# A sparse 3x3 convolution whose stores leave by two queues, one image each, with whole-pair loads and no tiny loads

## The chip, the cores and the metric

The kernel runs on one core of one Trainium2 chip. A core has five engines that run side by side: TensorE (PE in the profile, its weight loads PEld), VectorE (DVE), ScalarE (ACT), GpSimd (POOL) and SyncE (SP). Sixteen DMA engines carry data between the chip's memory (HBM) and the core's on-chip memory. SyncE, ScalarE and GpSimd can each issue transfers, by queues of their own. The metric is the device time of one execution in microseconds, taken as the median of several runs; one further execution is recorded by the hardware profiler, and all rows shown here come from such records.

## The reference

Sixteen images of 64 channels and 64x64 points are convolved with 128 filters of 3x3, padded by one. The weights are drawn with nine tenths of them zero, and the reference skips those; the kernel does the whole dense product.

```python
batch, c_in, h, w, c_out, k = 16, 64, 64, 64, 128, 3
x_pad = np.pad(x, ((0, 0), (0, 0), (1, 1), (1, 1)))
output[b, co] += weight[co, ci, kh, kw] * x_pad[b, ci, kh:kh+h, kw:kw+w]
```

The input is 16.8 MB of float32, the output 33.6 MB.

## The kernel before, in words

**Pairs and blocks.** Two images make a pair: 64 channels of each fill the 128 partitions. There are eight pairs (`NP`), and each is worked on in four blocks of 16 output rows (`BLOCKS`, `ROWS`), 32 blocks in all (`N`). Even and odd output rows of a block are formed from three partial products in the manner of Winograd along the rows: one product of `sums` (row pairs added), which both share, goes to `ps[0]`; one of `odd` to `ps[1]`; one of `even` to `ps[2]` or `ps[3]`. Each product is a run of matmuls with 64-row halves, one half for each image.

**Who does what.** GpSimd issues the loads of pairs (line 105; they turn float32 into bf16 on the way), then for each block adds row pairs (`fill_sums`, line 183) and copies the even rows (`fill_even`, line 172). ScalarE copies the shared product out of `ps[0]` into `pc` (line 280) and then the next block's odd rows (`fill_odd`, lines 163 and 164). VectorE adds `pc` to `ps[1]` and to `ps[2]` or `ps[3]` and so writes the even and odd output rows (lines 293 and 297) into one of four output buffers, `outs[p % 4]`. TensorE runs a loop over two blocks at a time (line 337 has all its products). Everything is ordered by semaphores set by hand: `s_pe` counts products, `s_pc` copies, `s_out` finished blocks, `s_x[p]` landed loads and `s_st[p]` landed stores of pair `p`.

**Loads.** The first 32 rows of pair 0 go by SyncE (line 94) beside the weights (line 91). The rest of pair 0 and pairs 1, 2 and 7 are one transfer each. Pairs 3 to 6 are three transfers: 59 to 62 of the rows, and the last two to five rows in two pieces divided by channel (`LOADS`). GpSimd issues pairs 0, 1, 2 and the first piece of pair 3 ahead of its blocks, and then one transfer from the list `todo` behind every filling step.

**Tiny loads.** SyncE waits until pair 2 has landed, then issues fifteen loads of 1 to 15 rows of 36 to 92 bytes of the weights into `spare`, which nothing reads (`marks`, line 305). It does so again behind pair 4's store (`MARKED`).

**Stores.** No store goes out before the load of pair 6 (`GATE`) has landed. Then SyncE goes through the pairs: it waits for a pair's four blocks and issues one 4 MB store with both images (line 320). Pairs 6 and 7 go in halves of 32 rows (`HALVED`); the last half of pair 7 is issued behind the section (line 370). Before VectorE writes pair `p` into a buffer again it waits until the store of pair `p - 4` has landed (line 290).

Of the kernel before, what the change touches and what calls it, by code (L numbers as in the profile page):

```python
# [7 lines left out]
FP32 = mybir.dt.float32  # L8
# [9 lines left out]
BLOCKS = 4  # L18
# [4 lines left out]
def kernel(  # L23
# [6 lines left out]
    nc = tc.nc  # L30
    B, C_IN, H, W = x.shape
    C_OUT, _, KH, KW = weight.shape
    assert (B, C_IN, H, W) == (16, 64, 64, 64) and (C_OUT, KH, KW) == (128, 3, 3)
    NP = B // 2
    HEAD = 32
    N = NP * BLOCKS
    GATE = 6
    HALVED = (6, 7)
    MARKED, MARKS = 4, tuple(range(1, 16))

    def sbuf(name, shape, dtype):
        return nc.alloc_sbuf_tensor(name, shape, dtype).ap()

    def sem(name):
        return nc.alloc_semaphore(name)

    def pair(p):
        return x[2 * p : 2 * p + 2].rearrange("n i h w -> (n i) h w")
# [5 lines left out]
    xs = [  # L54
        home[:, 1 + p, :].bitcast(BF16).rearrange("c (h w) -> c h w", w=W)
        for p in range(3)
    ]
    xs += [sbuf(f"x{p}", [128, H, W], BF16) for p in range(3, NP)]
    outs = [sbuf(f"o{k}", [C_OUT, 2, H, W], FP32) for k in range(3)]
# [1 line left out]
    w_sb = sbuf("w_sb", [C_OUT, C_IN * KH * KW], FP32)  # L61
    w_bf = sbuf("w_bf", [C_OUT, 3, 4 * C_IN], BF16)
    wT = sbuf("wT", [128, 5, 3, C_OUT], BF16)
    spare = sbuf("spare", [16, 2, 16, 32], FP32)
    ident = sbuf("ident", [128, 128], BF16)
    idle_rhs = sbuf("idle_rhs", [128, 512], BF16)
    zeros = idle_rhs[:, 0:W]
# [9 lines left out]
    s_x = [sem(f"s_x{p}") for p in range(NP)]  # L77
    s_st = [sem(f"s_st{p}") for p in range(NP)]
    s_dve, s_act, s_id, s_tr = sem("s_dve"), sem("s_act"), sem("s_id"), sem("s_tr")
    s_sum, s_even = ([sem(f"s_{n}{k}") for k in range(UNROLL)] for n in ("sum", "even"))  # L80
    s_odd, s_free, s_mark = sem("s_odd"), sem("s_free"), [sem(f"s_mark{i}") for i in range(2)]
    s_pe, s_pc, s_out = sem("s_pe"), sem("s_pc"), sem("s_out")

    def into(p, a, b):
        return out[2 * p : 2 * p + 2].rearrange("n o h w -> o n h w")[:, :, a:b, :]
# [8 lines left out]
    nc.sync.dma_start(out=x_head, in_=pair(0)[:, 0:HEAD, :]).then_inc(s_head, 16)  # L94

    LOADS = {p: [(0, H, 0, 128)] for p in range(NP)}
    LOADS[0] = [(HEAD, H, 0, 128)]
    for p, a, cut in ((3, 62, 120), (4, 60, 88), (5, 59, 117), (6, 61, 119)):  # L100
        LOADS[p] = [(0, a, 0, 128), (a, H, 0, cut), (a, H, cut, 128)]

    def load(p, i=0):
        a, b, c, d = LOADS[p][i]
        nc.gpsimd.dma_start(out=xs[p][c:d, a:b, :], in_=pair(p)[c:d, a:b, :]).then_inc(s_x[p], 16)  # L105

    load(0)
    nc.gpsimd.memset(ident, 0.0).then_inc(s_id, 1)
    nc.gpsimd.wait_ge(s_id, 1)
    nc.gpsimd.affine_select(  # L110
        out=ident,
        in_=ident,
# [8 lines left out]
    def source(p, r):  # L121
        if r < 0 or r >= H:
            return None, None
        if p == 0 and r < HEAD:
            return x_head, (s_head, 16)
        return xs[p], (s_x[p], 16 * len(LOADS[p]))

    def rows_of(k, first, count):

        p = k // BLOCKS  # L130
        pieces = []
        for i, r in enumerate(range(first, first + 2 * count, 2)):
            src, landed = source(p, r)
            if pieces and pieces[-1][2] is src:
                pieces[-1][1] += 1
                pieces[-1][4].append(landed)
            else:
                pieces.append([i, 1, src, r, [landed]])
        return sorted(pieces, key=lambda q: q[2] is not None)
# [3 lines left out]
    def wait(engine, s, value):  # L143
        key = (engine.engine, s.name)
        if waited.get(key, 0) < value:
            engine.wait_ge(s, value)  # L146
            waited[key] = value

    def fill(engine, copy, zero, tile_, k, first, count, done):
        for i, c, src, r, landed in rows_of(k, first, count):  # L150
            if src is None:
                last = zero(tile_[:, i, :])
            else:
                for s in landed:
                    wait(engine, *s)
                last = copy(tile_[:, i : i + c, :], src[:, r : r + 2 * c - 1 : 2, :])
        last.then_inc(done, 1)

    def fill_odd(k, engine=None, copy=None, zero=None, done=None):
        r0 = ROWS * (k % BLOCKS)  # L160
        fill(
            engine or nc.scalar,
            copy or (lambda o, i: nc.scalar.copy(out=o, in_=i)),  # L163
            zero or (lambda o: nc.scalar.copy(out=o, in_=zeros)),
            odd[k % UNROLL], k, r0 - 1, HALF + 1, done or s_odd,
        )
# [10 lines left out]
    def fill_sums(k, engine=nc.gpsimd):  # L177
        p, b = divmod(k, BLOCKS)
        r0 = ROWS * b
        src = source(p, r0)[0]  # L180
        for r in (r0, r0 + ROWS - 1):
            wait(engine, *source(p, r)[1])
        engine.tensor_tensor(  # L183
            out=sums[k % UNROLL],
            in0=src[:, r0 : r0 + ROWS : 2, :],
            in1=src[:, r0 + 1 : r0 + ROWS : 2, :],
            op=ADD,
        ).then_inc(s_sum[k % UNROLL], 1)
# [14 lines left out]
    v = nc.vector  # L203
# [21 lines left out]
    a = nc.scalar  # L225
# [35 lines left out]


    g = nc.gpsimd
    for p in (1, 2):
        load(p)
    todo = [(p, i) for p in range(3, NP) for i in range(len(LOADS[p]))]
    load(*todo.pop(0))
    for k in range(1, N):
        for fill_in, product in ((fill_sums, 2), (fill_even, 6)):
            if k >= UNROLL:  # L270
                wait(g, s_pe, 6 * (k - UNROLL) + product)
            fill_in(k)
            if todo:
                load(*todo.pop(0))


    fill_odd(0)
    for k in range(N):
        wait(a, s_pe, 6 * k + 2)
        a.copy(out=pc[k % 3], in_=ps[0]).then_inc(s_pc, 1)  # L280
        if k + 1 < N:
            fill_odd(k + 1)


    for k in range(N):
        p, b = divmod(k, BLOCKS)
        o = outs[p % 4]
        r0 = ROWS * b
        if p >= 4:
            wait(v, s_st[p - 4], 16)  # L290
        wait(v, s_pc, k + 1)
        wait(v, s_pe, 6 * k + 4)
        v.tensor_tensor(  # L293
            out=o[:, :, r0 : r0 + ROWS : 2, :], in0=ps[1], in1=pc[k % 3], op=ADD
        ).then_inc(s_free, 1)
        wait(v, s_pe, 6 * k + 6)
        v.tensor_tensor(  # L297
            out=o[:, :, r0 + 1 : r0 + ROWS : 2, :], in0=ps[2 + k % 2], in1=pc[k % 3], op=ADD
        ).then_inc(s_out, 1)


    s = nc.sync
    def marks(i, landed):
        for k in MARKS:
            s.dma_start(
                out=spare[0:k, i, k, 0 : 8 + k],
                in_=weight.rearrange("o i kh kw -> o (i kh kw)")[0:k, 0 : 8 + k],
            ).then_inc(landed, 16)

    s.wait_ge(s_x[2], 16)  # L310
    marks(0, s_mark[0])
    s.wait_ge(s_x[GATE], 16 * len(LOADS[GATE]))
    for p in range(NP):
        parts = 2 if p in HALVED else 1
        rows = H // parts
        for h in range(parts):
            if (p, h) == (NP - 1, 1):
                continue
            s.wait_ge(s_out, BLOCKS * p + BLOCKS // parts * (h + 1))
            s.dma_start(  # L320
                out=into(p, rows * h, rows * (h + 1)),
                in_=outs[p % 4][:, :, rows * h : rows * (h + 1), :],
            ).then_inc(s_st[p], 16)
        if p == MARKED:
            marks(1, s_mark[1])


    def tap(g, kw, n):
# [41 lines left out]
    nc.sync.dma_start(out=into(NP - 1, H // 2, H), in_=outs[(NP - 1) % 4][:, :, H // 2 : H, :])  # L370
    with tc.tile_critical(no_gpsimd_drain=True):
        for p in range(4, NP):
            s.wait_ge(s_st[p], 16)
        for m in s_mark:
            s.wait_ge(m, 16 * len(MARKS))


# [28 lines left out]
```

## Time and profile before

| | |
|---|---|
| median of 3 runs | 130.03 us (129.74 to 130.38) |
| the profiled execution | 130.27 us |
| its span, first to last instruction | 128.4 us |
| TensorE busy | 110.5 us |
| VectorE, ScalarE, GpSimd busy | 82.6, 54.5, 66.1 us |
| HBM read, written | 17.09 MB, 33.55 MB |

In a row of stretches the columns are the stretch in us, busy time and count for PE, PEld, DVE, ACT and POOL, the granted TensorE clock, the busy share of the DMA engines, and the GB/s that they wrote. A load counts there with the bf16 bytes that it writes, half of what it reads. In a timeline row the columns are start, length, engine, line, operation, result and source, form, count, and in brackets the engine's idle time ahead of it with what ended it; `SPq` stands for SyncE issuing a transfer. In a row of waits the columns are the total, how often, and the longest.

### The profile page before, as it was taken

What the parts mean: (1) busy time and instruction counts of PE and PEld (TensorE: products, weight loads), DVE (VectorE), ACT (ScalarE), POOL (GpSimd) and SP (SyncE); (2) the same over time, 40 slices, a digit from 0 to 9 for tenths busy, and PEclk for the clock granted to TensorE, in tenths of its full rate; (3) what the DMA queues carried; (4) which work ended last, traced back from release to release, by engine and by line L of the source; (5) the groups of instructions that cost most, each with busy time, mean ns of one, the idle gap of its engine ahead of it and who ended that gap; (6) DMA issues with size and microseconds to landing.
All of it is one profiled execution on the core that took longest, in us unless ns stands there. A gap on an engine that the chain in (4) does not pass through costs nothing.

```text
span 128.4 us, 2523 instructions
## 1 busy us (share of the span) xinstructions
PE 110.5 (86%) x983; PEld 57.0 (44%) x983; DVE 82.6 (64%) x74; ACT 54.5 (42%) x78; POOL 66.1 (51%) x93
## 2 busy tenths in 40 slices
PE   5999999999999999999999999999999999800000
PEld 2445555555555555555555555555555555300000
DVE  0577777777777777777777777777777777720000
ACT  3544545444544454445444544454445444300000
POOL 4479998875555555555555555555555550000000
PEclk9999999999999999999999999999999999996555
DMA  4999999999999999999999999999999999999920
GB/s 126 340 226 214 217 216 213 209 206 214 210 210 207 309 411 424 449 429 414 431 447 414 424 439 434 419 429 454 390 348 414 419 426 424 421 429 429 393 100 13
DMA packets 5348, 42.81 MB, mean 333 GB/s; under 512 B 1249, under 2 KB 1505, under 8 KB 2273
## 3 DMA queue, kind: packets, MB, share of 16 engines
q1 hardware_dynamic: 3488, 34.92, 65.3%
q0 software_dynamic: 1856, 7.87, 30.7%
q14 instruction: 4, 0.02, 0.0%
HBM read 17.09 MB, written 33.55 MB: 395 GB/s over the span
## 4 chain that ended last, share of the span: by engine, by line
PE 80%; DVE 2%; issue 0%; DVEq 0%
PE ps L337 80%; DVE home L293 1%; DVE home L297 1%; DVEq L146 0%
## 5 line engine op out<-in xcount | busy, mean ns | idle before, releaser
L280 ACT COPY pc<-ps 128x1024 f32<-128x1024 f32 x32 | 32.4, 1012 | 51.9 <-PE ps L337 51.9
L337 PE MATMUL ps<-even,wT 64*128 64x504 bf16 (+1 forms) x384 | 47.3, 377 | 0.0
L337 PE MATMUL ps<-odd,wT 64*128 64x504 bf16 (+1 forms) x384 | 47.3, 377 | 0.0
L293 DVE TENSOR_TENSOR o<-ps,pc 128x1024 f32<-128x1024 f32 x24 | 29.4, 1225 | 19.6 <-PE ps L337 19.6
L337 PEld LDWEIGHTS ps<-even,wT 64*128 64x128 bf16 x384 | 21.8, 94 | 19.7
L337 PEld LDWEIGHTS ps<-odd,wT 64*128 64x128 bf16 x384 | 21.8, 94 | 19.7
L297 DVE TENSOR_TENSOR o<-ps,pc 128x1024 f32<-128x1024 f32 x24 | 29.4, 1224 | 0.0
L337 PE MATMUL ps<-sums,wT 64*128 64x504 bf16 (+1 forms) x192 | 26.5, 377 | 0.1
L172 POOL COPY even<-x 128x576 bf16<-128x576 bf16 (+1 forms) x20 | 13.0, 650 | 21.4 <-PE ps L337 21.4
L183 POOL TENSOR_TENSOR sums<-x 128x512 bf16<-128x512 bf16 x20 | 23.1, 1154 | 0.0
L337 PEld LDWEIGHTS ps<-sums,wT 64*128 64x128 bf16 x192 | 10.8, 94 | 10.2 <-issue 0.5
L183 POOL TENSOR_TENSOR sums<-home 128x512 bf16<-128x512 bf16 (+1 forms) x11 | 13.4, 1214 | 2.6 <-DMA home<-in_x_dram 2.5
L293 DVE TENSOR_TENSOR home<-ps,pc 128x1024 f32<-128x1024 f32 x8 | 9.8, 1225 | 6.4 <-PE ps L337 6.4
L163 ACT COPY odd<-x 128x576 bf16<-128x576 bf16 (+1 forms) x20 | 13.2, 660 | 0.0
L297 DVE TENSOR_TENSOR home<-ps,pc 128x1024 f32<-128x1024 f32 x8 | 9.8, 1224 | 0.0
L172 POOL COPY even<-home 128x576 bf16<-128x576 bf16 (+2 forms) x11 | 6.8, 614 | 5.2 <-PE ps L337 5.2
L105 POOL DMA_DIRECT2D x<-in_x_dram x13 | 7.1, 544 | 0.0
L239 PE MATMUL ps<-idle_rhs 128*128 128x512 bf16 x14 | 5.5, 564 | 1.4 <-DVE idle_rhs L204 1.4
L163 ACT COPY odd<-home 128x576 bf16<-128x576 bf16 (+1 forms) x10 | 6.6, 657 | 0.0
L173 POOL MEMSET even<- 128x64 bf16 x8 | 1.2, 154 | 9.4 <-PE ps L337 9.4
L239 PEld LDWEIGHTS ps<-idle_rhs 128*128 128x128 bf16 x14 | 1.8, 137 | 3.8 <-issue 2.2
L200 DVE CAST w_bf<-w_sb 128x192 bf16<-128x192 f32 (+1 forms) x4 | 1.1, 351 | 2.5 <-DMA w_sb<-in_weight_dram 2.5
(21 smaller groups left out, 15.2 us busy)
## 6 DMA issues: line engine op xcount, KB each, us to landing
out_dram<-o SPq DMA_DIRECT2D x5, 4096.0 KB, 21.4
out_dram<-home SPq DMA_DIRECT2D x1, 4096.0 KB, 23.8
out_dram<-o SPq DMA_DIRECT2D x2, 2048.0 KB, 17.6
out_dram<-home SPq DMA_DIRECT2D x2, 2048.0 KB, 14.6
home<-in_x_dram POOLq DMA_DIRECT2D x2, 1024.0 KB, 12.9
home<-in_x_dram SPq DMA_DIRECT2D x1, 1024.0 KB, 5.7
x<-in_x_dram POOLq DMA_DIRECT2D x1, 1024.0 KB, 21.8
x<-in_x_dram POOLq DMA_DIRECT2D x1, 992.0 KB, 19.0
```

Of the source, the lines that this page charges most:

```text
L105: nc.gpsimd.dma_start(out=xs[p][c:d, a:b, :], in_=pair(p)[c:d, a:b, :]).then_inc(s_x[p], 16)
L163: copy or (lambda o, i: nc.scalar.copy(out=o, in_=i)),
L172: copy or (lambda o, i: nc.gpsimd.tensor_copy(out=o, in_=i)),
L173: zero or (lambda o: nc.gpsimd.memset(o, 0.0)),
L183: engine.tensor_tensor(out=sums[k % UNROLL], in0=src[:, r0 : r0 + ROWS : 2, :], in1=src[:, r0 + 1 : r0 + ROWS : 2, :], op=ADD,).then_inc(s ...
L200: copy(out=w_bf4[:, g, a:b, :], in_=w_v[:, k : k + b - a, :]).then_inc(done, 1)
L239: t.matmul(idle_ps, idle_rhs[:, 0:128], idle_rhs, start=True, stop=True)
L280: a.copy(out=pc[k % 3], in_=ps[0]).then_inc(s_pc, 1)
L293: v.tensor_tensor(out=o[:, :, r0 : r0 + ROWS : 2, :], in0=ps[1], in1=pc[k % 3], op=ADD).then_inc(s_free, 1)
L297: v.tensor_tensor(out=o[:, :, r0 + 1 : r0 + ROWS : 2, :], in0=ps[2 + k % 2], in1=pc[k % 3], op=ADD).then_inc(s_out, 1)
L337: mm = t.matmul(into[:, n, :, c_lo:c_hi], tap(g, kw, n), src[q, i : i + HALF, c_lo + kw - 1 : c_hi + kw - 1], start=(m == 0), stop=(m == l ...
```

## The change

Each store becomes two transfers of one image each. SyncE issues image 0 and ScalarE image 1; both count on `s_st[p]`, so the reuse of a buffer waits for 32 in place of 16. ScalarE issues its stores in its block loop, from block `FIRST` = 10 on, behind the copy of the next block's odd rows, and only where the additions of the store's blocks come from blocks before the current one. At block 10 it first waits for the load of pair 6, as SyncE does. Only the last half of pair 7 is still one transfer of both images by SyncE. Each pair is loaded in one transfer; GpSimd issues pairs 1, 2 and 3 ahead of its blocks, and 4 to 7 behind its next four filling steps. The tiny loads, their buffer, semaphores and final waits are gone.

```diff
-    LOADS = {p: [(0, H, 0, 128)] for p in range(NP)}
-    LOADS[0] = [(HEAD, H, 0, 128)]
-    for p, a, cut in ((3, 62, 120), (4, 60, 88), (5, 59, 117), (6, 61, 119)):
-        LOADS[p] = [(0, a, 0, 128), (a, H, 0, cut), (a, H, cut, 128)]
+    def load(p):
+        a = HEAD if p == 0 else 0
+        nc.gpsimd.dma_start(out=xs[p][:, a:H, :], in_=pair(p)[:, a:H, :]).then_inc(s_x[p], 16)
...
-    for p in (1, 2):
+    for p in (1, 2, 3):
         load(p)
-    todo = [(p, i) for p in range(3, NP) for i in range(len(LOADS[p]))]
-    load(*todo.pop(0))
+    todo = list(range(4, NP))
...
+    PARTS = []
+    for p in range(NP):
+        n = 2 if p in HALVED else 1
+        PARTS += [(p, H // n * h, H // n * (h + 1), BLOCKS * p + BLOCKS // n * (h + 1)) for h in range(n)]
+    PARTS.pop()
+
+    def store(engine, part, n):
+        p, a, b, _ = part
+        engine.dma_start(
+            out=out[2 * p + n][:, a:b, :], in_=outs[p % 4][:, n, a:b, :]
+        ).then_inc(s_st[p], 16)
+
+    parts = list(PARTS)
     fill_odd(0)
     for k in range(N):
         wait(a, s_pe, 6 * k + 2)
         a.copy(out=pc[k % 3], in_=ps[0]).then_inc(s_pc, 1)
         if k + 1 < N:
             fill_odd(k + 1)
+        if k == FIRST:
+            wait(a, s_x[GATE], 16)
+        while k >= FIRST and parts and parts[0][3] <= k:
+            wait(a, s_out, parts[0][3])
+            store(a, parts.pop(0), 1)
...
         if p >= 4:
-            wait(v, s_st[p - 4], 16)
+            wait(v, s_st[p - 4], 32)
...
-    s.wait_ge(s_x[2], 16)
-    marks(0, s_mark[0])
-    s.wait_ge(s_x[GATE], 16 * len(LOADS[GATE]))
-    for p in range(NP):
...
-            s.dma_start(
-                out=into(p, rows * h, rows * (h + 1)),
-                in_=outs[p % 4][:, :, rows * h : rows * (h + 1), :],
-            ).then_inc(s_st[p], 16)
-        if p == MARKED:
-            marks(1, s_mark[1])
+    s.wait_ge(s_x[GATE], 16)
+    for part in PARTS:
+        wait(s, s_out, part[3])
+        store(s, part, 0)
```

More of the change, by code (lines that the diff above doesn't have):

```diff
@@ L38 @@
     HALVED = (6, 7)
-    MARKED, MARKS = 4, tuple(range(1, 16))
+    FIRST = 10
     def sbuf(name, shape, dtype):
@@ L63 @@
     wT = sbuf("wT", [128, 5, 3, C_OUT], BF16)
-    spare = sbuf("spare", [16, 2, 16, 32], FP32)
     ident = sbuf("ident", [128, 128], BF16)
@@ L80 @@
     s_sum, s_even = ([sem(f"s_{n}{k}") for k in range(UNROLL)] for n in ("sum", "even"))
-    s_odd, s_free, s_mark = sem("s_odd"), sem("s_free"), [sem(f"s_mark{i}") for i in range(2)]
+    s_odd, s_free = sem("s_odd"), sem("s_free")
     s_pe, s_pc, s_out = sem("s_pe"), sem("s_pc"), sem("s_out")
@@ L94 @@
     nc.sync.dma_start(out=x_head, in_=pair(0)[:, 0:HEAD, :]).then_inc(s_head, 16)
-    LOADS = {p: [(0, H, 0, 128)] for p in range(NP)}
-    LOADS[0] = [(HEAD, H, 0, 128)]
-    for p, a, cut in ((3, 62, 120), (4, 60, 88), (5, 59, 117), (6, 61, 119)):
-        LOADS[p] = [(0, a, 0, 128), (a, H, 0, cut), (a, H, cut, 128)]
-    def load(p, i=0):
-        a, b, c, d = LOADS[p][i]
-        nc.gpsimd.dma_start(out=xs[p][c:d, a:b, :], in_=pair(p)[c:d, a:b, :]).then_inc(s_x[p], 16)
+    def load(p):
+        a = HEAD if p == 0 else 0
+        nc.gpsimd.dma_start(out=xs[p][:, a:H, :], in_=pair(p)[:, a:H, :]).then_inc(s_x[p], 16)
     load(0)
@@ L125, in source @@
             return x_head, (s_head, 16)
-        return xs[p], (s_x[p], 16 * len(LOADS[p]))
+        return xs[p], (s_x[p], 16)
     def rows_of(k, first, count):
@@ L273 @@
             if todo:
-                load(*todo.pop(0))
+                load(todo.pop(0))
+    PARTS = []
[9 more added lines that the diff above has]
+    parts = list(PARTS)
     fill_odd(0)
@@ L302 @@
     s = nc.sync
[L303 to L308, printed above, removed]
-    s.wait_ge(s_x[2], 16)
-    marks(0, s_mark[0])
-    s.wait_ge(s_x[GATE], 16 * len(LOADS[GATE]))
-    for p in range(NP):
[L314 to L320, printed above, removed]
-                out=into(p, rows * h, rows * (h + 1)),
-                in_=outs[p % 4][:, :, rows * h : rows * (h + 1), :],
-            ).then_inc(s_st[p], 16)
-        if p == MARKED:
-            marks(1, s_mark[1])
+    s.wait_ge(s_x[GATE], 16)
+    for part in PARTS:
+        wait(s, s_out, part[3])
+        store(s, part, 0)
     def tap(g, kw, n):
@@ L372 @@
         for p in range(4, NP):
-            s.wait_ge(s_st[p], 16)
-        for m in s_mark:
-            s.wait_ge(m, 16 * len(MARKS))
+            n = sum(part[0] == p for part in PARTS)
+            s.wait_ge(s_st[p], 32 * n)
 _INS = ['x', 'weight']
```

## The prediction

> **What bounds the kernel now.** I read the page first (slices and HBM line), then the chain of waits, then stretches of the span with the transferred rate, and last the issues of SyncE's queue.
>
> ```profile
> span 128.4 us, 2523 instructions
> ...
> DMA  4999999999999999999999999999999999999920
> GB/s 126 340 226 214 217 216 213 209 206 214 210 210 207 309 411 424 449 429 414 431 447 414 424 439 434 419 429 454 390 348 414 419 426 424 421 429 429 393 100 13
> ...
> HBM read 17.09 MB, written 33.55 MB: 395 GB/s over the span
> ```
>
> The DMA row is at nine tenths or more in every slice from the second to the third from last. The rate row has two levels: about 213 GB/s while loads run (they turn float32 into bf16, so what is written is half of what HBM gives, and 213 written is 426 read) and about 428 while stores run. Both are one and the same ceiling. (17.09 + 33.55) MB at 428 GB/s takes 118 us of the 128.4, so transfers bound this kernel, and what counts is whatever leaves the DMA engines idle or makes them finish unevenly.
>
> ```profile
> 8.00 102.64 PE ps L337 x948
> ...
> 111.96 1.22 DVE home L297
> ```
>
> The chain of waits ends with the last addition at 113.18. Fifteen of the 128.4 us follow it, and in these only stores run:
>
> ```profile
> 113.47 0.37 SPq L370 DMA_DIRECT2D out_dram<-home  x1
> ```
> ```profile
> 112.00:118.00 6.00, 0.00 (x0) 0.00 (x0) 1.19 (x1) 0.00 (x0) 0.00 (x0) 0.85 1.01 425
> ...
> 120.00:121.00 1.00, 0.00 (x0) 0.00 (x0) 0.00 (x0) 0.00 (x0) 0.00 (x0) 0.50 1.04 442
> 121.00:122.00 1.00, 0.00 (x0) 0.00 (x0) 0.00 (x0) 0.00 (x0) 0.00 (x0) 0.50 0.68 287
> 122.00:123.00 1.00, 0.00 (x0) 0.00 (x0) 0.00 (x0) 0.00 (x0) 0.00 (x0) 0.50 0.46 197
> 123.00:124.00 1.00, 0.00 (x0) 0.00 (x0) 0.00 (x0) 0.00 (x0) 0.00 (x0) 0.50 0.21 90
> 124.00:125.00 1.00, 0.00 (x0) 0.00 (x0) 0.00 (x0) 0.00 (x0) 0.00 (x0) 0.50 0.08 33
> 125.00:126.00 1.00, 0.00 (x0) 0.00 (x0) 0.00 (x0) 0.00 (x0) 0.00 (x0) 0.50 0.06 25
> 126.00:127.00 1.00, 0.00 (x0) 0.00 (x0) 0.00 (x0) 0.00 (x0) 0.00 (x0) 0.50 0.04 16
> ```
>
> The last two columns are DMA share and GB/s. At 113.47 a backlog is still queued: the engines stay full for 7.5 us more. Then the rate falls in steps, and from 124.5 to 126.6 it is 25 GB/s, one sixteenth of 428 less a little: a single engine works alone. After 121 the sixteen engines move 648 KB, which at 428 takes 1.5 us, so if evenly loaded they would end near 122.5 and not at 126.6. The end of the kernel is the last engine's end, 4.1 us behind an even finish.
>
> **Removed: the tiny loads (L305).** Thirty go, fifteen before the first store and fifteen behind pair 4's.
>
> ```profile
> 18.68 5.27 SPq L305 DMA_DIRECT2D spare<-in_weight_dram  x15
> 39.00 9.75 SPq L320 DMA_DIRECT2D out_dram<-o  x3
> ...
> 74.31 0.37 SPq L320 DMA_DIRECT2D out_dram<-o  x1
> 74.73 15.78 SPq L305 DMA_DIRECT2D spare<-in_weight_dram  x15
> 90.55 10.07 SPq L320 DMA_DIRECT2D out_dram<-o  x3
> ```
> ```profile
> 70.00:80.00 10.00, 10.00 (x96) 5.26 (x94) 7.59 (x7) 4.84 (x7) 5.73 (x8) 1.00 1.00 426
> 80.00:90.00 10.00, 10.00 (x96) 5.28 (x94) 7.59 (x7) 4.92 (x8) 5.72 (x8) 1.00 1.02 434
> 90.00:100.00 10.00, 10.00 (x96) 5.24 (x93) 7.62 (x7) 5.11 (x8) 5.73 (x8) 1.00 1.00 393
> ```
>
> The second fifteen hold SyncE for 15.78 us, 1.05 each against 0.35 for the first fifteen. The four blocks of pair 5 take 12.97 us (102.64 / 32 = 3.21 a block on TensorE, so about 12.9), so pair 5's store, due that long after 74.31, near 87.3, goes out at 90.55. Around it the rate dips: 393 against 430, the mean of the two stretches before, is 37/430 of 10 us = 0.86 us of all engines lost. With the marks gone this goes. Bounds: 0 (the last engine, which sets the end, lost nothing) and 15/7.5 of it, 1.7 us (marks go to 1 to 15 rows, so if one row goes to one engine some get fifteen and some none, mean 7.5). Without a per-engine row I take the mean, **-0.86**. The first fifteen run beside loads and are counted with those.
>
> **Changed: one transfer per pair (L105).**
>
> ```profile
> 24.00:28.00 4.00, 1.00 1.10 209
> ...
> 32.00:36.00 4.00, 1.00 1.06 210
> ```
> ```profile
> 12.00:15.00 3.00, 1.00 1.02 213
> ```
> ```profile
> L105 POOL DMA_DIRECT2D x<-in_x_dram x13: 502/547/579, 4.1 to 25.1; - x13
> ```
>
> SyncE's marks at 18.68 began when pair 2 had landed, and its first store at 39.00 when pair 6 had: four pairs in 20.32 us. A pair is 1.049 MB written; at the unsplit 213 GB/s four take 19.69. That is 0.63 us for the eight extra small pieces and the first marks. By rates alone (209.5 against 213, the span of 20.3 us) it is 0.33. I take the middle, **-0.5**; ends 0 and -0.63, as a last landing may wait on one engine. POOL issues eight loads fewer at 0.547 us, 4.4 us. That is worth nothing: TensorE, unbroken from 8.00, never waited for POOL. Loads go out earlier, which is no gain either as the load queue never ran dry (no slice before 40 falls below nine tenths but the first).
>
> **Moved: the second image's stores to ScalarE's queue (L320).** One issue becomes two of half the bytes, ten stores become nineteen transfers.
>
> ```profile
> L320 SPq DMA_DIRECT2D out_dram<-o x7: 372/406/470, 39.0 to 100.2; - x7
> ```
> ```profile
> 41.29 1.01 ACT L280 COPY pc<-ps 128x1024 f32<-128x1024 f32 x1 [1.66 <-PE ps L337]
> 42.20 0.67 ACT L163 COPY odd<-home 128x576 bf16<-128x576 bf16 x1
> 44.53 1.01 ACT L280 COPY pc<-ps 128x1024 f32<-128x1024 f32 x1 [1.66 <-PE ps L337]
> ```
>
> No row shows a ScalarE issue; nearest is SyncE's 0.406 us. Block 10's pc copy is the one at 41.29 and its odd copy ends at 42.87. There ScalarE now waits for pair 6 (landed by 39.00) and for additions already done, and issues two stores, 0.81 us, inside the 1.66 us it idled for TensorE. Queued behind them is only block 11's pc copy. Later blocks carry one issue or none. If an issue is held up as the marks were (1.05 us), the two take 2.1, and pc slips 0.45 us; the additions shift with it once. Even so the last store would be issued later than 113.47 into a backlog 7.5 us deep. Cost taken: 0; ends 0 and 0.45, with no gain.
>
> The extra transfers themselves: 4 MB stores run at 431 GB/s, 2 MB ones (112 to 118) at 425.
>
> ```profile
> 50.00:60.00 10.00, 10.00 (x96) 5.26 (x94) 7.62 (x7) 4.84 (x7) 5.46 (x7) 1.00 1.01 431
> ```
>
> That is 1.4% of 4.9 us, 0.07 us a transfer, and nine more make 0.6. But those 2 MB stores also have half-length rows (8 KB), which pairs 0 to 5 keep at 16 KB, so I take **+0.2**, ends 0 and +0.6.
>
> On this a page of the Trainium skill speaks against the change. "DMA: Bandwidth & Descriptors", section "Anatomy of one DMA — SWDGE (gpsimd) path", gives about 2.0 us fixed for each transfer beside its bytes, for the GpSimd path. Nine more would then be 18 us if paid in line, 130.0 - 1.2 + 18 = 147 us, an estimate by that page; the trace disagrees with paying it in line, as 425 GB/s across a border of queued 2 MB stores leaves no room for 2 us in 5.
>
> **Added waits.** An output buffer is used again after both halves have landed (L290's wait, now for 32).
>
> ```profile
> 62.14 1.23 DVE L293 TENSOR_TENSOR o<-ps,pc 128x1024 f32<-128x1024 f32 x1 [0.82 <-PE ps L337]
> ```
> ```profile
> out_dram<-o SPq DMA_DIRECT2D x5, 4096.0 KB, 21.4
> ```
>
> Block 16 is the first, at 62.14. ScalarE's half of pair 0 is issued at about 42.9 behind SyncE's two halves at 39. At 2.1 MB a half and 428 GB/s, the rest of load 7 (at most 4.9 us), SyncE's two halves and this one are 19.6 us of work from 39: done by 58.6 at worst, 3.5 us early. Later pairs have more room, since 9.8 us of work arrives every 12.9. Queued behind that wait would be every addition, and TensorE through ps1; I take 0, and 1 us as upper end.
>
> **Sum.** Against the profiled execution's 130.27: -0.86 - 0.5 + 0.2 = -1.16, 129.1 us; the median of the runs is 0.24 lower, so **128.9**. With the ends: -2.3 to +2.0, that is 127.7 to 132.0. About 0.5% (0.65 us) is what a measurement of this kernel can tell from no change.
>
> **Rivals.**
>
> *A, the uneven finish goes too.* If marks and unequal load pieces made the engines uneven, the end also gains the 4.1 us: 128.9 - 4.1 = 124.8. For it: pieces of 1 to 15 rows are unequal by construction. Against it: their bytes are tiny, and the whole dip is 0.86 us a mean engine. Chance 0.12.
>
> *B, a second queue's start costs what the first one's did.* When the stores joined the loads, the rate fell:
>
> ```profile
> 40.00:42.00 2.00, 1.00 1.25 205
> 42.00:44.00 2.00, 1.00 0.76 229
> 44.00:46.00 2.00, 1.00 1.05 438
> ```
>
> These 4 us write 0.87 MB. If load 7 ran from about 36.7 at 0.212 MB per us, 0.35 MB of it were left at 40, so HBM moved 0.70 + 0.52 = 1.22 MB of a possible 1.72: 1.1 us lost. Paid once more at ScalarE's first issue: 130.0, no change. Against it: no load is left to mix with by then. Chance 0.19.
>
> *C, the last engine gets later.* If unevenness builds up per transfer (4.1 us over ten stores), nineteen make up to 3.7 us more: 132.6, slower. Place: the tail after 121; it decides from 1.16 + 0.65 = 1.8 us more. For it: two queues' rows take turns on each engine and nothing equalises the engines. Against: bytes per engine don't change. Chance 0.20.
>
> *D, each turn between queues costs.* The dip's 0.86 x 16 engines over 120 mark rows is 0.115 us an interruption. An engine moves 33.55 MB / 16 in about 160 rows; if nearly every one were a switch, 150 x 0.115 = 17 us: 146. It decides from 1.8 / 150 = 12 ns. Against it: 438 GB/s at 44 to 46 with load rows still among the stores. Chance 0.06, with the 2 us a transfer.
>
> **How the numbers follow.** My forecast 0.43, A 0.12, B 0.19, C 0.20, D 0.06. Faster 0.55 (forecast and A), same 0.19 (B), slower 0.26 (C and D). The range 126.6 to 132.2 leaves out most of A, D and C's far end, 0.2 together; the likeliest case alone is 128.1 to 129.4.
>
> **What would show it.** No dip near 90 to 100 (rate at 425 or more); pair 5's store at about 87.5; SyncE's first store at about 38.5; ScalarE's idle before block 11's pc copy shorter by 0.8 and TensorE unbroken; the tail still one engine long. I am wrong if the store stretch runs below 420 with both queues filled, if the tail after the last full stretch changes by more than a microsecond, or if an addition waits for an output.

## The result and the profile after

The changed kernel takes 128.74 us (median of 3 runs, 128.56 to 128.75) where the kernel before takes 130.03. The ratio is 0.9895, with a 95% interval of 0.9853 to 0.9936. The forecast was 128.9. A later series with more runs (below) gave 128.69 us and 0.9903, 0.9875 to 0.9931. The profiled execution took 128.56 us, with a span of 126.7 against 128.4.

First the page of the changed kernel, the same lines as before: the span, the DMA engines' share and the GB/s in 40 slices, and what HBM moved.

```profile
span 126.7 us, 2494 instructions
...
DMA  3999999999999999999999999999999999999930
GB/s 85 369 221 215 217 215 220 209 215 220 212 222 204 248 445 429 424 429 432 434 424 419 445 424 429 414 429 445 424 429 429 416 422 427 429 424 427 429 145 10
...
HBM read 17.07 MB, written 33.55 MB: 400 GB/s over the span
```

The dip to 390 and 348 in slices 29 and 30 is gone; the store stretch now holds 414 to 445 to its end. Next SyncE's issues, in order of time, and the chain of waits:

```profile
38.35 10.62 SPq L277 DMA_DIRECT2D out_dram<-o  x3
...
113.73 0.39 SPq L363 DMA_DIRECT2D out_dram<-home  x1
```
```profile
87.53 6.82 SPq L277 DMA_DIRECT2D out_dram<-o  x2
```
```profile
8.25 102.64 PE ps L330 x948
...
112.22 1.23 DVE home L309
```

The first store goes out at 38.35 in place of 39.00, and pair 5's at 87.53 in place of 90.55. TensorE takes 102.64 us as before, in one piece. The end, in stretches of one microsecond (last columns: DMA share, GB/s):

```profile
120.00:121.00 1.00, 0.00 (x0) 0.00 (x0) 0.00 (x0) 0.00 (x0) 0.00 (x0) 0.50 1.04 442
121.00:122.00 1.00, 0.00 (x0) 0.00 (x0) 0.00 (x0) 0.00 (x0) 0.00 (x0) 0.50 0.36 148
122.00:123.00 1.00, 0.00 (x0) 0.00 (x0) 0.00 (x0) 0.00 (x0) 0.00 (x0) 0.50 0.06 25
123.00:124.00 1.00, 0.00 (x0) 0.00 (x0) 0.00 (x0) 0.00 (x0) 0.00 (x0) 0.50 0.06 25
124.00:125.00 1.00, 0.00 (x0) 0.00 (x0) 0.00 (x0) 0.00 (x0) 0.00 (x0) 0.50 0.06 25
```

Fifteen engines now finish almost together, between 121 and 122; before, they straggled to 124. The sixteenth still works alone for three microseconds at 25 GB/s. Its last packet ends at 125.05, where it ended at 126.74.

### The profile page after: what moved, and what is told of

Read it like the earlier page. It is cut to its first block, busy times and chain, and to the rows that moved or that the text cites. A ratio compares the mean times of both kernels' runs of the same rounds, so it can differ in the third digit from the quotient of the medians.

```text
span 126.7 us, 2494 instructions
## 1 busy us (share of the span) xinstructions
PE 110.4 (87%) x983; PEld 57.3 (45%) x983; DVE 82.7 (65%) x74; ACT 54.6 (43%) x78; POOL 62.2 (49%) x85
## 4 chain that ended last, share of the span: by engine, by line
PE 84%; DMA 3%; DVE 2%; issue 0%; SPq 0%; DVEq 0%
PE ps L330 81%; DMA w_sb<-in_weight_dram 3%; PE ps L232 2%; PE ps L236 1%; DVE home L309 1%; DVE home L305 1%; DVE w_bf L193 0%; SPq L393 0%; DVEq L139 0%; SPq L87 0%
## 5 line engine op out<-in xcount | busy, mean ns | idle before, releaser
L98 POOL DMA_DIRECT2D x<-in_x_dram x5 | 2.8, 551 | 0.0
```

Of the source, the lines that this page charges most:

```text
L98: nc.gpsimd.dma_start(out=xs[p][:, a:H, :], in_=pair(p)[:, a:H, :]).then_inc(s_x[p], 16)
```

## The experiments

**The change taken apart: four kernels.** The change has three parts. Each was undone or done alone.

```diff
 e1_no_tiny_loads: the kernel before, and
-    s.wait_ge(s_x[2], 16)
-    marks(0, s_mark[0])
...
-        if p == MARKED:
-            marks(1, s_mark[1])
...
 e2_whole_loads: the kernel before, and
-    for p, a, cut in ((3, 62, 120), (4, 60, 88), (5, 59, 117), (6, 61, 119)):
-        LOADS[p] = [(0, a, 0, 128), (a, H, 0, cut), (a, H, cut, 128)]
 e3_one_queue: both of these
 e4_two_queues_only: the kernel before, its stores by SyncE and ScalarE
...
+        while k >= 10 and parts and parts[0][3] <= k:
+            wait(a, s_out, parts[0][3])
+            store(a, parts.pop(0), 1)
...
```

> The kernel before without the thirty tiny loads; split pair loads and the one store queue stay. My theory (the tiny loads cost the 0.86 us of the dip, the split loads 0.5 us, the second queue adds 0.2 us): 129.2 us, no dip at 90 to 100 us, pair 5's store issued near 87.5 us. Rival (the gain comes from the two store queues): 130.0 us. Second rival (the end is one slow engine that the tiny loads hardly touch): 129.7 to 130.0 us with the dip gone all the same.

> The kernel before with one transfer per pair; the thirty tiny loads and the one store queue stay. My theory: 129.5 us, first store issued near 38.5 us in place of 39.0. Rival (gain from the two store queues): 130.0 us.

> The kernel before with whole-pair loads and without tiny loads, stores still one transfer of both images by SyncE: the change without its second queue. My theory: 128.5 us, a little under the changed kernel's 128.74 (the second queue adds 0.2 us, at most 0.6). Rival (gain from the two store queues): 130.0 us.

> The kernel before with its stores split over SyncE's and ScalarE's queues, nothing else changed: tiny loads and split pair loads stay, and SyncE issues the second tiny loads behind pair 4's first image. My theory: 130.2 us, up to 130.6. Rival (gain from the two store queues): 128.7 us.

| kernel | tiny loads | pair loads | store queues | us | ratio to before (95%) |
|---|---|---|---|---|---|
| before | yes | split | one | 130.03 | 1 |
| e1 | no | split | one | 128.28 | 0.9868 (0.9847 to 0.9888) |
| e2 | yes | whole | one | 130.10 | 1.0009 (0.9994 to 1.0024) |
| e3 | no | whole | one | 128.41 | 0.9874 (0.9855 to 0.9893) |
| e4 | yes | split | two | 129.07 | 0.9932 (0.9911 to 0.9953) |
| after | no | whole | two | 128.74 | 0.9895 (0.9853 to 0.9936) |

The tiny loads are worth 1.75 us alone and 1.69 with whole loads (e2 to e3), twice what I had put on them. Whole loads are worth nothing: +0.07 with the tiny loads, +0.13 without. The second queue costs 0.33 us where no tiny loads are left (e3 to after, though the intervals overlap). Where they are left it *gains* 0.96 us (before to e4), which no theory on record had at that size: mine said 130.2, the rival 128.7.

Why whole loads gain nothing shows at the turn from loads to stores. The stretches 40 to 42 and 42 to 44 us, first of e1 (split loads), then of e3 (whole), last column GB/s:

```profile
40.00:42.00 2.00, 2.00 (x22) 1.04 (x19) 2.00 (x2) 0.43 (x1) 1.05 (x3) 1.00 1.06 184
42.00:44.00 2.00, 2.00 (x22) 1.08 (x20) 1.21 (x2) 1.16 (x2) 0.77 (x1) 1.00 0.92 287
```
```profile
40.00:42.00 2.00, 2.00 (x22) 1.02 (x18) 2.00 (x2) 0.39 (x1) 1.01 (x3) 1.00 1.15 168
42.00:44.00 2.00, 2.00 (x22) 1.04 (x20) 1.21 (x2) 1.20 (x2) 0.81 (x1) 1.00 0.84 266
```

The first store goes out half a microsecond earlier with whole loads (38.49 against 38.98 us), but the turn then writes 0.87 MB in four microseconds where the split loads' turn writes 0.94. The trace's packets, GpSimd's loads counted with the bytes that they read, say how much that is: by 40 us e3 has moved 16.01 MB and e1 15.90, by 44 us both have moved 17.4. The lead of 0.11 MB, 0.26 us at 428 GB/s, is given back in the turn; how, the traces don't tell.

Why the second queue gains beside tiny loads: with one queue, pair 5's whole store stands behind them, and the stretch from 90 to 100 us has 393 GB/s in the kernel before. It is not that SyncE issues this store late, at 90.55. In e2, first below, it goes out at 87.45, the rate is 393 all the same, and nothing is gained. In e4, below it, the stretch keeps 419:

```profile
87.45 13.26 SPq L318 DMA_DIRECT2D out_dram<-o  x3
```
```profile
90.00:100.00 10.00, 10.00 (x96) 4.55 (x94) 7.62 (x7) 5.11 (x8) 5.73 (x9) 1.00 1.00 393
```
```profile
90.00:100.00 10.00, 10.00 (x96) 5.32 (x94) 7.62 (x7) 5.11 (x8) 5.73 (x9) 1.00 1.01 419
```
```profile
87.33 0.34 ACTq L285 DMA_DIRECT2D out_dram<-o  x1
```

ScalarE issues its half of pair 5 at 87.33, in a queue that holds no tiny loads. The packets show the effect: of the 16 KB store packets that start between 85 and 100 us, 17 take over 700 ns in the kernel before and 17 in e2, but 3 in e4; 611 is usual. So the second queue spares the engines most of the stalls that the next experiment traces to the tiny loads. That this makes up all of the 0.96 us isn't shown.

**Which tiny loads.** Each set alone, on e3.

```diff
 e5_second_tiny_only                    e6_first_tiny_only
+        if p == MARKED:                +    s.wait_ge(s_x[2], 16)
+            marks(1, s_mark[1])        +    marks(0, s_mark[0])
...                                     ...
```

> Whole-pair loads and one store queue, with only the second fifteen tiny loads (behind pair 4's store). Theory S (they stand in the store stream ahead of pair 5's rows and hold up the last engine there, the first fifteen are free): 130.0 us, as with both sets. Rival (each set costs its share, half of 1.7 us): 129.2 us.

> Whole-pair loads and one store queue, with only the first fifteen tiny loads (during the loads). Theory S: 128.4 us, as with none. Rival (each set costs its share): 129.2 us.

The second set alone: 129.94 us, ratio 0.9977 (0.9954 to 0.9999). The first alone: 128.78 us, 0.9894 (0.9859 to 0.993). Beside e3's 0.9874, the second set costs 1.0% (1.3 us) and the first 0.2% (0.3 us, inside the intervals). It is the set in the store stream that hurts, and it hurts even where SyncE isn't late: here pair 5's store went out at 87.42.

How can 120 rows of 36 to 92 bytes cost the last engine 1.3 us? The trace's packets, which the views don't list one by one, can be told apart here: the fifteen sizes differ, and an engine's first size says which of the sixteen it is, if the rows of a transfer are dealt out in order. The late engine's first tiny packet has 52 bytes, so it is the fifth by that order, in the kernel before and in e2; in kernels without tiny loads nothing tells which one it is. Behind its last tiny packet:

```text
start ns  took ns  bytes      (kernel before; a 16384-byte store packet takes 611 elsewhere)
95251     12       92
95265     1402     16384
96653     654      16384
97304     1209     16384
```

The tiny packets take 11 or 12 ns each. Of the store packets behind them the first takes 1402 ns and the third 1209, where most of this engine's others take 625 to 662: 1.3 us in all. The late engine isn't the only one hit. In the kernel before, the engines with one to four tiny rows need 611 or 612 ns for each of the six store packets that follow; the one with all fifteen has packets of 1859 and 1195 among its first three; the late one has eleven rows. So the stall grows with the number of tiny rows ahead of an engine's store rows. A packet of 4 bytes comes with each tiny one; which of the two holds the stores up, and how, isn't shown. The landing events of the stores, in us from the first instruction, say the same for the whole engine:

```text
landings, us: earliest / last engine    pair 3's store    pair 4's store    pair 5's store    last store
before                                  81.46 / 85.19     91.26 / 95.69     101.80 / 107.36   121.79 / 127.17
e3_one_queue                            82.29 / 84.78     92.00 / 95.06     101.74 / 105.38   121.31 / 125.34
e7_half_matmuls                         82.33 / 83.93     92.07 / 93.99     101.77 / 104.06   121.37 / 123.89
e12_half_columns                        82.49 / 85.16     92.21 / 95.60     101.94 / 105.34   121.52 / 124.83
```

From pair 4's store to pair 5's the last engine takes 11.67 us before and 10.32 in e3: 1.35 us, which is what the second set costs in e5.

**Why one engine is late at all.** In the table it needs 10.28 us from pair 3's store to pair 4's in e3, where the earliest engine needs 9.71. It loses 0.57 us, and about as much from pair 4's to pair 5's (10.32 for 9.74). TensorE's instructions were the suspect, as the most numerous.

```diff
 e7_half_matmuls, on e3
-                mm = t.matmul(into[:, n, ...], tap(g, kw, n), src[q, ...], ...)     # for n in range(2)
+            mm = t.matmul(into[:, m % 2, :, :], wT[:, g, kw, :], src[:, i : i + HALF, :], ...)
...
 e12_half_columns, on e3
+            half = slice(64 * (m % 2), 64 * (m % 2) + 64)
+                mm = t.matmul(into[half, n, :, :], tap(g, kw, n)[:, half], src[q, i : i + HALF, :], ...)
...
```

> Whole-pair loads, no tiny loads, one store queue; TensorE issues one matmul over all 128 rows where it issued two over 64, into the two images' banks by turns, so half as many matmuls and weight loads at about the same pace. The sums are not the convolution any more; only the amount of instructions is the point. Theory I (the one late engine is slowed by TensorE's instructions being fetched): the stretch in which one engine works alone at the end (about 3 us in the kernel with one queue) shrinks to about half or less. Theory N (the lateness has nothing to do with TensorE's instructions): it stays at about 3 us. A slower TensorE would move the end but not the answer, as long as the stores still queue.

> Whole-pair loads, no tiny loads, one store queue; as many matmuls and weight loads as in the kernel before, but each makes 64 of the 128 output rows, by turns, so the weights read and the sums written are half. The output is not the convolution any more. Theory I (the late engine follows the number of TensorE's instructions): one engine works alone at the end for about 3 us, as with whole matmuls, and 128.4 us if TensorE keeps its pace. Rival (it follows what TensorE reads and writes, which the run with half the matmuls halved on the writing side): the stretch shrinks to 1.5 us and 126.9 us.

Neither computes the convolution any more, and each was run once: 126.87 us and 127.89 us. In e12 TensorE didn't keep its pace, so its time falls between the two expectations and can't be read directly; the rate of instructions can. Stretches of e3, e7 and e12 (PE's busy time with its count of matmuls is the first pair):

```profile
60.00:70.00 10.00, 10.00 (x96) 5.28 (x94) 7.60 (x7) 4.75 (x6) 5.46 (x7) 1.00 0.99 423
```
```profile
90.00:100.00 10.00, 9.90 (x46) 4.51 (x46) 7.63 (x7) 5.13 (x8) 5.75 (x8) 1.00 0.99 424
```
```profile
60.00:70.00 10.00, 8.18 (x123) 3.65 (x119) 8.89 (x8) 6.18 (x10) 7.08 (x10) 1.00 1.00 428
...
80.00:90.00 10.00, 7.84 (x120) 3.48 (x112) 9.19 (x9) 6.34 (x9) 7.29 (x9) 1.00 1.01 429
...
100.00:110.00 10.00, 0.00 (x0) 0.00 (x0) 0.00 (x0) 0.00 (x0) 0.00 (x0) 0.50 0.99 420
```

From pair 3's store to pair 4's, the late engine loses 0.57 us with 96 matmuls in 10 us, 0.32 with 46, and 0.72 with 116 from 85 to 95 us (10.44 - 9.72). In e12 the compute is over by 95 us, and from pair 4's store to pair 5's the late engine takes 9.74 us beside 9.73 for the earliest: it isn't slow any more. The bytes read and written don't fit: e12 writes half into PSUM and loads half the weights per matmul, and loses more; e7 reads 46 times 128 input rows in ten microseconds where e3 reads 96 times 64, nearly as many, and loses little more than half. Nor do the other engines' instructions, 7, 8 and 8 in e7's row beside 7, 6 and 7 in e3's. So the lateness follows the rate of TensorE's instructions, in one profiled execution of each of three kernels. That the engine carries these instructions to TensorE would explain it but isn't shown; the page counts only three packets of the queue called instruction.

At the end, the rate from 122 to 128 us, first e3, then e7, then e12:

```profile
122.00:128.00 6.00, 0.00 (x0) 0.00 (x0) 0.00 (x0) 0.00 (x0) 0.00 (x0) 0.50 0.04 15
```
```profile
122.00:128.00 6.00, 0.00 (x0) 0.00 (x0) 0.00 (x0) 0.00 (x0) 0.00 (x0) 0.57 0.01 5
```
```profile
122.00:128.00 6.00, 0.00 (x0) 0.00 (x0) 0.00 (x0) 0.00 (x0) 0.00 (x0) 0.50 0.03 11
```

90, 30 and 66 KB are left then, not all of them of one engine. By the landing events the last engine is alone for 2.4 us in e3, 1.5 in e7 and 2.4 in e12. For e7 that is shorter, if not the half of the expectation; for e12 it is as long as in e3, as the first theory had it, though its lateness stops growing at 95 us.

**Relieving the late engine: three attempts, all misses.**

```diff
 e8_first_four, on e3
+                for o in range(112, 128, 4):
+                    s.dma_start(out=dst[o : o + 4, few], in_=src[o : o + 4, few]).then_inc(s_st[p], 16)
+                s.dma_start(out=dst[0:112], in_=src[0:112]).then_inc(s_st[p], 16)
...
 e9_skip_fifth, on e3
+    LOADS[3] = [(0, H, 0, 5), (0, H, 5, 125), (0, H, 125, 128)]
 e10_skip_last, on e3
+    LOADS[3] = [(0, H, 0, 120), (0, H, 120, 128)]
```

> Whole-pair loads, no tiny loads, one store queue; of the second half of pair 6 (one image) and the first half of pair 7 (both images) the last 16 channels are stored by transfers of four channels each. Theory (a transfer of four rows uses four engines, none of them the late one, and so takes one row of every sixteen from it): the late engine ends 0.9 us earlier and the four take 2.7 us more without becoming the last: 127.5 us against 128.4. Rival (other engines become last, or the small transfers cost more than they move): 128.4 us or more.

> Whole-pair loads but for pair 3, no tiny loads, one store queue. Pair 3 is loaded as 5, 120 and 3 partitions. Theory (GpSimd's transfers of fewer than 16 equal shares go to consecutive engines, each starting where the last one stopped, so the 120 partitions miss just the fifth engine, the late one): the late engine has 6 of its 8 rows of this pair less, about 3.6 us, and the end comes some 2.5 us earlier, 126.0 us, with the stretch of a single engine at the end nearly gone. Rival (the shares go elsewhere): 128.4 us or later, with the single engine's stretch as before.

> The same, but pair 3 is loaded as 120 and 8 partitions. Theory: the 120 miss the sixteenth engine, not the late one; the single engine's stretch stays and the time is 128.4 us (the eight other rows may add up to 0.6 us to some engines, the late one among them or not). Rival (any uneven load helps): under 127.5 us.

e8 took 134.1 us in the median of six executions (132.1 to 137.3). The ratio counts the three fastest, 132.1 to 133.5 us: 1.0208 (1.0146 to 1.027). SyncE's issues and the stretch behind them show why:

```profile
101.54 3.54 SPq L323 DMA_DIRECT2D out_dram<-o  x4
...
108.02 6.32 SPq L323 DMA_DIRECT2D out_dram<-home  x4
```
```profile
112.00:118.00 6.00, 1.20 (x12) 0.39 (x8) 2.45 (x2) 0.00 (x0) 0.00 (x0) 0.85 0.51 164
```

Four small issues took 3.5 and then 6.3 us where one of a whole store takes 0.37, the store behind them was late, and the engines stood half idle at 164 GB/s. The small transfers cost far more than they moved.

e9 took 128.88 us (0.9933, 0.9907 to 0.996) and e10 129.33 us (0.9948, 0.993 to 0.9967), both above e3, e10 by more than its expectation allowed. The theory in e9 failed: some engine did miss pair 3's rows (one engine's part of pair 4's load landed at 23.57 us, the others' from 27.85 on), but it was another than the late one, which landed last as before, at 126.05. The lead also didn't last. It was 4.9 us at pair 7's load and 1.2 us at the first store, because no stores are issued before 39 us. So even a well aimed load could not have bought the late engine more than that.

**The changed kernel again.**

> The changed kernel once more with more rounds. Theory (the second queue costs a little, as against the same kernel with one queue at 128.41 us): 128.7 us. Rival (no difference between one and two queues): 128.4 us.

128.69 us, ratio 0.9903 (0.9875 to 0.9931), against e3's 0.9874 (0.9855 to 0.9893). The second queue's 0.3 us is seen in both series of the changed kernel, but the intervals overlap.

The kernels e1 and e3 are faster than both the kernel before and the changed one in their medians: 128.28 and 128.41 us. Of the three parts of the change only the missing tiny loads are a gain.

## Why the prediction was right, and where it wasn't

*The bound.* That transfers bound the kernel and that its end is the last engine's end held in every run with whole stores: in e12 the compute is over by 95 us, and the kernel still takes 127.89. The gain in the profiled executions, 1.71 us, is the last engine's, 126.74 to 125.05 us.

*The sum.* -1.16 forecast, -1.29 measured between the medians: right in size, but of terms that were not. The tiny loads were put at -0.86 and measured -1.7; whole loads at -0.5 and measured +0.1; the second queue at +0.2 and measured +0.3. The first two errors cancel. So the total is right by luck. The step that failed is "without a per-engine row I take the mean": the tail's rows had already said that one engine alone sets the end, and what counts is the stall of that engine. It has eleven of the 120 tiny rows where the mean engine has 7.5, and 11/7.5 of 0.86 is 1.26 us; the second set measured 1.3, and the late engine's step 11.67 us for 10.32. That both sets together come to the upper bound of 1.7 is chance: the bound was worked out for an engine with fifteen rows, and the rest of the 1.7 is the first set's 0.3, inside its intervals. The -0.5 of the loads was a true saving of 0.5 to 0.65 us at the first store (39.00 to 38.35), but was counted as if nothing followed; the turn from loads to stores took it back.

*The signs.* The dip, both store times and the single engine at the end came as said. But one sign of being wrong came too: behind the last full stretch, which ends at 121 in both kernels, the tail is 1.69 us shorter, where I had allowed one. The gain lies in that tail, on the last engine, and not in what the mean engine lost in the dip.

*Where the tiny loads act.* I counted the first fifteen with the loads and the second with the dip. e5 and e6 agree that the second set is the dear one.

*ScalarE.* The cost of its issues was put at nothing, in the idle time behind the odd copy. The cost was right and the place wrong. The changed kernel's ScalarE around block 10:

```profile
41.55 1.01 ACT L287 COPY pc<-ps 128x1024 f32<-128x1024 f32 x1 [1.66 <-PE ps L330]
41.61 2.18 ACTq L277 DMA_DIRECT2D out_dram<-o  x2
42.46 0.68 ACT L156 COPY odd<-home 128x576 bf16<-128x576 bf16 x1
44.79 1.01 ACT L287 COPY pc<-ps 128x1024 f32<-128x1024 f32 x1 [1.66 <-PE ps L330]
```

The two issues begin while the copy ahead of them still runs, 0.06 us after its start, and overlap both copies. The idle time before block 11's pc copy is 1.66 us, not 0.8 shorter as I had said. The pair takes 2.18 us, 1.76 for the longer one, more than the 2.1 of my upper end, and still delays nothing.

*The added wait.* No addition waited for an output. Block 16's, the first to use a buffer again, starts at 62.39 with the 0.82 us of idle time ahead of it that it had before, and the wait is for TensorE:

```profile
62.39 1.22 DVE L305 TENSOR_TENSOR o<-ps,pc 128x1024 f32<-128x1024 f32 x1 [0.82 <-PE ps L330]
```

*The rivals.* A, that the uneven finish goes, came half true and shows why it was worth nothing: fifteen engines now end together, but the sixteenth stays. B, a cost at the second queue's start, is of the size of the 0.3 us at most, where 1.1 was its price. C is refuted: unevenness does not build up per transfer, since the single engine's stretch is no longer with nineteen transfers (three stretches of 25 GB/s, 75 KB after 122 us) than with ten (90 KB in e3), and what makes that engine late goes with TensorE's rate of instructions. D is refuted by 425 to 431 GB/s in each ten microseconds with both queues full:

```profile
60.00:70.00 10.00, 10.00 (x96) 5.28 (x93) 7.60 (x7) 4.75 (x6) 5.47 (x7) 1.00 1.01 431
...
90.00:100.00 10.00, 10.00 (x96) 5.32 (x94) 7.63 (x7) 4.95 (x8) 5.74 (x9) 1.00 1.00 426
```

The same rows answer the page "DMA: Bandwidth & Descriptors" of the Trainium skill, section "Anatomy of one DMA — SWDGE (gpsimd) path": its fixed 2 us of each transfer, by estimate 18 us for nine more, is not paid in line where transfers queue on these two paths.

## What to carry to other kernels

Where sixteen DMA engines finish unevenly, a stall is priced on the last of them and not on the mean, by what that one engine has in its queue: look at the rate in the last microseconds, and when it is one sixteenth, ask what each edit does to that one engine. Time saved ahead of a change of traffic, loads to stores here, isn't saved until the far side of it is looked at. And a sum that comes out right may rest on two errors; only kernels that do one part alone tell.

## What was not expected of the hardware

One of the sixteen engines, the fifth by the order of rows in the kernel before and in e2, stores about 6% slower than the others as long as TensorE runs (10.28 us for 9.71 in a 4 MB step in e3). What it loses goes with the number of matmuls that TensorE issues (0.32, 0.57 and 0.72 us at 46, 96 and 116 in ten us), and it stores at full rate once TensorE has stopped (9.74 for 9.73 in e12). Eleven tiny reads ahead of a stream of stores lengthen two of the store packets behind them by 1.3 us together on that engine, and up to four do nothing. Small transfers of fewer rows than engines are slow to issue while stores are queued: 0.3 to 2.5 us each in e8, about 1.05 for the tiny loads behind pair 4's store in the kernel before and 0.35 for those beside the loads, against 0.37 for a whole store. ScalarE issues a transfer while its copies ahead of it in the program still run (41.61, beside a copy from 41.55 to 42.56).
